# Modulation and the compressed keys' first layer as products on quarters of TensorE's array, and all rests on VectorE, in a two-block network on one core

## The chip, the cores and the metric

One core of a Trainium2 chip runs the whole program in one launch. TensorE multiplies matrices (PE, its weight loads PEld), VectorE (DVE), ScalarE (ACT) and GpSimd (POOL) work element by element, and SyncE (SP) issues the loads. The metric is the device time of one execution in microseconds, the median of the runs.

## The reference

256 tokens of width 1024 go through two blocks. Only the first one is touched here. In it a condition vector `c` is turned into six modulation vectors by one product of a vector with a matrix of 1024 x 6144 (24 MB):

```
cond = silu(c)
mod = cond @ ada_w + ada_b
sh1, sc1, g1, sh2, sc2, g2 = split(mod, 6)
h = rms_norm(x, ln1_g) * (1 + sc1) + sh1
x = x + g1 * hybrid_mixer(h, w_in, w_out, ...)
h = rms_norm(x, ln2_g) * (1 + sc2) + sh2
x = x + g2 * sparse_moe(h, ...)            # 32 experts, 4 per token
```

So `sc1` and `sh1` are needed ahead of everything, `g1` at the output projection, `sc2` and `sh2` at the routing, `g2` at the end of the experts. The mixer holds two kinds of attention over the same projection `w_in`. One of them attends, among others, to compressed keys and values: 31 windows (two groups of 15, and the position vectors as one more column) of 32 x 64 numbers each go through `gelu(flat @ w1) @ w2`, with `w1` of 2048 x 128, once for keys and once for values.

All is fp32. A dense product of activations and weights is made of three products of rounded parts, hi x hi, hi x lo and lo x hi.

## The kernel before, in words

**Weights.** Class `Stream` loads 1 MB tiles of weights in one fixed list order (`add`, `pump`; the load is L170). The list is written by hand at the head of the kernel: `add_ada(s, q)` puts a quarter (256 rows by 1024 columns) of section `s` of `ada_w` into it, `more(n)` the next `n` quarters of the sections that are not yet in it. There are four places of 1 MB and some more in stretches (`widen`). A load can start when the tile that was in its place, and all tiles ahead of that one, are used. A tile of dense weights is cut into two units; `split_to` makes each unit's hi part on ScalarE (L190) and its rest, lo, by a subtraction (L192) on GpSimd or VectorE; the letters of `st.cut` say which, in turn. `st.ahead` says how many units ahead this is done. Modulation's tiles are used as they are (`get_raw`).

**Order on the engines.** Each engine runs its instructions in the order in which the program writes them. A dense step `dense_t` writes 24 products (three per 128 rows of weights: L290, L291, L292) into one bank `dps`, and between them pops other work: attention steps (`self.bg`, by `fill`) and one part of the side list `self.side` (by `aux`); `side_to(n)` writes parts until `n` are left. A part of the side list that needs a tile is not popped before its load is written.

**Modulation (`ada`).** Per section eight parts, one for each 128 rows of `ada_w`. VectorE multiplies a row of 1024 columns per partition by that partition's condition and adds it up in `acc` (L435 the first, L437 the others); in some parts ScalarE multiplies (L429, L557) and GpSimd adds (L431, L560). Then two totals: four transposes of 128 columns on TensorE (L449), a sum over their columns on VectorE (L452), and the addition to the bias (L454). Sections 1 and 0 come ahead of the first dense product (with an extra form of the last quarter, L592); the other four are the side list and go on until the second half of the output projection, where `side_to` writes what is left.

**Compressed keys.** `hid_part` multiplies, in eight background steps of four products (L660), 128 x 128 weights with 31 columns of the windows.

**Stages on the time line:** start to 41.2 us; two dense steps for the compressed keys and values and six for queries and keys of the first kind of attention, to 80; gates and values to 94; eight dense steps for queries and keys of the second kind with attention between them (L727, L741 norms; L830, L834 scores; L837 to L859 softmax; L866 transposes into the banks `tp` and `m`; L877 and L880 values, L880 for two heads in the upper and the lower 64 partitions of one bank), to 158; two steps of values to 190; output projection (`w_out_half`, eight banks each, with the update of h, L949, after each bank), first half to 217, second with the routing's products (L1032, L1035) to 250; routing to 263; the experts (first product L1441) to 1208; the second block to the end.

The lines 1914 and 1915, in the second block, are two products inside a loop over two heads, so that the program writes L1914, L1915, L1914, L1915; the two heads write the upper and the lower 64 partitions of one bank:

```
for a in range(2):
    hs = slice(64 * a, 64 * a + 64)
    mm(ot[hs, META:NT], lhsT=v[:, 64 * a:64 * a + 64], rhs=wa[:, a], ...)          # L1914
    mm(ot[hs, META + 128:NT], lhsT=v[:, 128 + 64 * a:192 + 64 * a], rhs=wb[:, a], ...)  # L1915
```

Of the kernel before, what the change touches and what calls it, by code (L numbers as in the profile page):

```python
# [20 lines left out]
S = 256  # L21
# [222 lines left out]
class Ker:  # L244
# [116 lines left out]
    def queue_pre(self):  # L361
# [14 lines left out]
        for s in (1, 0):  # L376
            for q in range(4):
                add_ada(s, q)
        add_cols(st, w, 512, 256)
        cw = A["nsa_cmp_w1"][0]  # L380
        for c in range(2):
# [4 lines left out]
                    for m in range(2)])  # L386
            st.add([(lambda t, b=b: t.rearrange("p (l h) -> p l h", l=16)[64 * b:64 * b + 64],
                     cw[c, 1024 * b:1024 * b + 1024].rearrange("(l d) h -> d l h", d=64)) for b in range(2)], ["raw"])
        for o in (768, 896):
# [5 lines left out]
            more()  # L395
        self.early = len(st.items)
        for c in range(4):
            add_cols(st, w, 1304 + 256 * c, 256)
            more(2 - c % 2)
        for c in range(2):  # L400
            st.add([(_v("p (k n) -> p k n", k=8), w[:, 2328 + c * 256:2584 + c * 256].rearrange("(k p) n -> p k n", p=128))],
                   [lambda t, m=m: t[:, m * 1024:m * 1024 + 1024] for m in range(2)])
            more()
        wo = A["w_out"][0]
        for c in range(2):
# [4 lines left out]
            more()  # L410
        for c in range(2):
            add_half(st, wo[:, c * 512:c * 512 + 512], 512, 512)
        more(len(rest))

    def ada(self, s, acc, pool, tag, first=0):

        nc = self.nc
        accs = [acc]

        def part(k):  # L420
            def go():
                if k % 2 == 0:
                    self.ada_t = self.st.get_raw()
                t, used = self.ada_t
                w = t[:, (k % 2) * 1024:(k % 2) * 1024 + 1024]
                if k in (1, 3, 5) and self.mid is not None:

                    b, t = self.mid[:, 0], self.mid[:, 1]
                    nc.scalar.activation(out=t if len(accs) > 1 else b, in_=w, func=AF.Copy, scale=self.cond[:, k:k + 1])  # L429
                    if len(accs) > 1:  # L430
                        nc.gpsimd.tensor_tensor(out=b, in0=b, in1=t, op=ALU.add)  # L431
                    else:
                        accs.append(b)
                elif k == first:
                    nc.vector.tensor_scalar(out=acc, in0=w, scalar1=self.cond[:, k:k + 1], scalar2=None, op0=ALU.mult)  # L435
# [7 lines left out]
        def total(i):  # L443
            def go():
                ps = pool.tile([128, 512], F32, name="adat", tag=tag)
                if len(accs) > 1:
                    nc.vector.tensor_tensor(out=acc, in0=acc, in1=accs.pop(), op=ALU.add)
                for m in range(4):
                    nc.tensor.transpose(ps[:, m * 128:m * 128 + 128], acc[:, i * 512 + m * 128:i * 512 + m * 128 + 128],  # L449
                                        self.c("ident"))  # L450
                t = self.pp.tile([128, 4], F32, name="adas", tag="adas", bufs=2)
                nc.vector.tensor_reduce(out=t, in_=ps.rearrange("p (m n) -> p m n", m=4), axis=AX.X, op=ALU.add)  # L452
                m4 = self.mod[:, 8 * s + 4 * i:8 * s + 4 * i + 4]
                nc.vector.tensor_tensor(out=m4, in0=t, in1=m4, op=ALU.add)  # L454
            return go

        return [part(k) for k in range(8)] + [total(i) for i in range(2)]
# [42 lines left out]
    def pre(self):  # L500
# [4 lines left out]
        with ExitStack() as ctx:  # L505
# [39 lines left out]
            self.mid = None  # L545
# [1725 lines left out]
```

## Time and profile before

| | us |
|---|---|
| median of 3 runs | 1894.74 (1891.46 to 1902.87) |
| profiled execution | 1895.64 |
| its span | 1893.8 |
| TensorE busy | 1776.0 (94%) |
| VectorE busy | 991.1 (52%) |
| ScalarE busy | 632.8 (33%) |
| GpSimd busy | 410.2 (22%) |
| TensorE's mean granted clock | 0.976 |

The span runs from the first to the last instruction. A busy share over the whole span mixes stages with different limits, so the stretches of the rows below are to be read one by one. A granted clock of 1.00 is TensorE's higher level (2.4 GHz), 0.50 its lower one (1.2 GHz). One fp32 product is two records of TensorE (two passes).

### The profile page before, as it was taken

To read this page: it belongs to the slowest core of one execution; us is meant where nothing else is said; L and a number is where in the kernel's file an instruction comes from. 1 tells how busy PE (TensorE), PEld (TensorE's weight loads), DVE (VectorE), ACT (ScalarE), POOL (GpSimd) and SP (SyncE) were. 2 spreads that over 40 slices of the span, in tenths; PEclk is the share of its full clock that TensorE was granted. 3 is DMA by queue.
4 is the path that set the end of the run, shared out by engine and by line. 5 is a ranking of instruction groups with operands and counts; after the bars stand their busy time and mean duration, and the time that the engine had idled before them with its cause. 6 is when DMAs were issued, how large, how long until landed. Compare 5 with 4: busy or idle time off the path is not lost. (4 is left out here: it accounts for less than half of the span.)

```text
span 1893.8 us, 25887 instructions
## 1 busy us (share of the span) xinstructions
PE 1776.0 (94%) x10035; PEld 1107.9 (58%) x10035; DVE 991.1 (52%) x1617; ACT 632.8 (33%) x1110; POOL 410.2 (22%) x269
## 2 busy tenths in 40 slices
PE   3988779999999999999999999799999999889998
PEld 2866643333334343333434333377779999889986
DVE  7686744544444433444443444545566543996622
ACT  3444322111211101121110112346565544756633
POOL 4533310000000000000000000164433344554443
PEclk6999989999999999999999999899999999999999
DMA  9544789999999999999999999552245545346552
GB/s 342 205 149 135 251 326 370 424 425 424 424 425 423 425 425 401 424 424 425 423 426 424 400 424 424 222 175 74 74 134 175 182 157 178 112 128 181 181 188 79
DMA packets 183342, 549.60 MB, mean 290 GB/s; under 512 B 8656, under 2 KB 101968, under 8 KB 150256
## 3 DMA queue, kind: packets, MB, share of 16 engines
q1 hardware_dynamic: 182592, 545.99, 74.5%
q0 software_dynamic: 432, 1.57, 0.3%
q8 instruction: 80, 1.31, 0.3%
q10 hardware_dynamic: 192, 0.35, 0.1%
q14 instruction: 46, 0.38, 0.1%
HBM read 546.83 MB, written 1.05 MB: 289 GB/s over the span
## 5 line engine op out<-in xcount | busy, mean ns | idle before, releaser
L192 POOL TENSOR_TENSOR wsp<-wraw,wsp 128x1024 fp32r<-128x1024 f32 x137 | 337.1, 2465 | 1383.8 <-PE cb L1568 964.6
L190 ACT CAST wsp<-wraw 128x1024 fp32r<-128x1024 f32 x208 | 215.4, 1044 | 108.8 <-PE f L2184 46.9
L290 PE MATMUL dps<-hn_hi,wsp 128*128 128x272 f32 (+1 forms) x816 | 242.8, 297 | 9.5 <-DVE h L1935 4.1
L291 PE MATMUL dps<-hn_lo,wsp 128*128 128x272 f32 (+1 forms) x816 | 237.1, 291 | 4.0 <-DVE hn_lo L1637 4.0
L292 PE MATMUL dps<-hn_hi,wsp 128*128 128x272 f32 (+1 forms) x816 | 237.4, 291 | 0.8 <-DVE wsp L192 0.8
L1572 DVE SCALAR_TENSOR_TENSOR h<-cb,vec,h 128x256 f32<-128x256 f32 x256 | 111.8, 479 | 227.5 <-PE cb L1568 227.5
L1441 PE MATMUL u<-wraw_s,xs 128*64 128x512 f32 x728 | 208.5, 602 | 0.9 <-DVE gl L1471 0.9
L1469 ACT COPY gl<-u 64x512 f32<-64x512 f32 x120 | 66.8, 583 | 418.0 <-PE u L1441 357.0
L1441 PE MATMUL u<-wraw,xs 128*64 128x512 f32 x648 | 195.2, 604 | 0.0
L290 PEld LDWEIGHTS dps<-hn_hi,wsp 128*128 128x128 f32 x816 | 157.4, 193 | 14.7 <-issue 5.8
L1441 PE MATMUL u<-wraw_r,xs 128*64 128x512 f32 x544 | 164.4, 608 | 0.0
L291 PEld LDWEIGHTS dps<-hn_lo,wsp 128*128 128x128 f32 x816 | 157.3, 193 | 5.4 <-DVE hn_lo L1637 4.7
L292 PEld LDWEIGHTS dps<-hn_hi,wsp 128*128 128x128 f32 x816 | 157.3, 193 | 1.1 <-DVE wsp L192 1.1
L1471 DVE TENSOR_TENSOR gl<-u,gl 64x512 f32<-64x512 f32 x120 | 79.1, 680 | 140.9 <-ACT gl L1469 140.9
L192 DVE TENSOR_TENSOR wsp<-wraw,wsp 128x1024 fp32r<-128x1024 f32 x71 | 91.2, 1287 | 90.6 <-ACT wsp L190 90.5
L1441 PEld LDWEIGHTS u<-wraw_s,xs 128*64 128x64 f32 x728 | 54.7, 136 | 75.4 <-issue 66.2
L2035 DVE TENSOR_TENSOR y<-r 128x272 f32<-128x272 f32 (+1 forms) x64 | 53.5, 835 | 62.6 <-ACT r L2032 62.6
L1441 PEld LDWEIGHTS u<-wraw,xs 128*64 128x64 f32 x648 | 49.5, 136 | 60.4 <-issue 51.5
L1543 PE MATMUL y<-wraw_s,at 128*64 128x512 f32 x368 | 82.8, 594 | 0.0
L1543 PE MATMUL y<-wraw_r,at 128*64 128x512 f32 x336 | 78.0, 605 | 3.7 <-SPq L1246 3.7
L1567 PE MATMUL cb<-st,y 128*128 128x256 f32 x256 | 80.2, 336 | 0.1
L1510 ACT COPY at<-at_ps 128x512 f32<-128x512 f32 x34 | 19.9, 587 | 176.9 <-PE at_ps L1508 176.9
(514 smaller groups left out, 3325.4 us busy)
## 6 DMA issues: line engine op xcount, KB each, us to landing
wraw_s<-in_exp_w SPq DMA_DIRECT2D x147, 1024.0 KB, 14.3
wraw_r<-in_exp_w SPq DMA_DIRECT2D x120, 1024.0 KB, 15.4
wraw<-in_exp_w SPq DMA_DIRECT2D x117, 1024.0 KB, 14.1
wraw<-in_mlp_w_up SPq DMA_DIRECT2D x32, 1024.0 KB, 5.4
wraw<-in_mlp_w_down SPq DMA_DIRECT2D x32, 1024.0 KB, 4.8
wraw<-in_ada_w SPq DMA_DIRECT2D x18, 1024.0 KB, 5.9
wraw<-in_sb_w_qkv SPq DMA_DIRECT2D x12, 1024.0 KB, 4.9
wraw<-in_lru_w_in SPq DMA_DIRECT2D x8, 1024.0 KB, 5.0
```

The lines of the kernel that those rows point to most:

```text
L190: nc.scalar.copy(out=hv, in_=src)
L192: e.tensor_tensor(out=lv, in0=src, in1=lr, op=ALU.subtract)
L290: mm(o, lhsT=wh, rhs=xh, start=first, stop=False)
L291: mm(o, lhsT=wh, rhs=xl, start=False, stop=False)
L292: mm(o, lhsT=wl, rhs=xh, start=False, stop=last)
L1441: mm(u[n][64 * j:64 * j + 64], lhsT=xs[:, k, o:o + 64], rhs=w[:, ns], start=(q == 0), stop=(q == 3))
L1469: nc.scalar.copy(out=o, in_=u[n][64:128])
L1471: nc.vector.tensor_tensor(out=o, in0=u[n][R], in1=o, op=ALU.add)
L1543: mm(y[n][64 * j:64 * j + 64], lhsT=at[:, k, 0:64], rhs=w[:, ws], start=(q == 0), stop=(q == 3))
L1567: mm(o, lhsT=yh[:, m * 128:m * 128 + 128], rhs=st, start=True, stop=False)
L1572: nc.vector.scalar_tensor_tensor(out=h[:, m, META:NT], in0=o, scalar=self.mod[:, 40 + m:41 + m], in1=h[:, m, META:NT], op0=ALU.mult, op1=A ...
L2035: nc.vector.tensor_tensor(out=y[:, :n], in0=r[:, :n], in1=r[:, :n], op=ALU.mult)
```

## The change

Each tile of modulation becomes eight products on TensorE instead of sums on VectorE. The condition of 128 rows, one column repeated 32 times, is the stationary side, 256 columns of the tile are the moving side, and the output goes to one of four quarters (32 partitions) of one bank. Two rows of weights per tile and four column blocks make eight products. VectorE then copies or adds the 256 columns into `acc`. A total is two small products with a choice matrix that picks one partition of each quarter. The compressed keys' first layer gets the same form: the windows are the stationary side (32 columns), `w1` the moving side (128 columns), the sixteen products go round the four quarters, and a product with `sel` adds the quarters up and turns them. All rests of the first block go to VectorE. In the load order the first `w_in` tile comes between sections 1 and 0, the compressed keys' `w1` after `w_in`'s fifth tile, and the side sections earlier; all side parts are written before the output projection. The norm of the start moves from GpSimd to VectorE.

```diff
-        for s in (1, 0):
-            for q in range(4):
-                add_ada(s, q)
+        for q in range(4):
+            add_ada(1, q)
         add_cols(st, w, 512, 256)
+        for q in range(4):
+            add_ada(0, q)
...
-            more()
+            for c in range(2):
+                if o == 768:
+                    st.add([(lambda t, b=b: t.rearrange("p (l h) -> p l h", l=16)[64 * b:64 * b + 64],
+                             cw[c, 1024 * b:1024 * b + 1024].rearrange("(l d) h -> d l h", d=64)) for b in range(2)], ["raw"])
+        more(3)
         self.early = len(st.items)
         for c in range(4):
             add_cols(st, w, 1304 + 256 * c, 256)
-            more(2 - c % 2)
+            more(3 - c // 2)
...
-        def part(k):
+        def part(q):
             def go():
-                if k % 2 == 0:
-                    self.ada_t = self.st.get_raw()
-                t, used = self.ada_t
-                w = t[:, (k % 2) * 1024:(k % 2) * 1024 + 1024]
...
-                    nc.vector.scalar_tensor_tensor(out=acc, in0=w, scalar=self.cond[:, k:k + 1], in1=acc,
-                                                   op0=ALU.mult, op1=ALU.add)
-                if k % 2:
-                    used()
+                t, used = self.st.get_raw()
+                if q == 0 or not whole:
+                    st["ps"] = bank("adap")
+                ps = st["ps"][:, 0:256]
+                for i in range(2):
+                    c = self.cond[:, 2 * q + i:2 * q + i + 1].to_broadcast([128, 32])
+                    for j in range(4):
+                        o = i * 1024 + j * 256
+                        nc.tensor.matmul(ps[32 * j:32 * j + 32], lhsT=c, rhs=t[:, o:o + 256],
+                                         start=(i == 0 and (q == 0 or not whole)), stop=(i == 1 and (q == 3 or not whole)))
+                used()
+                if whole and q < 3:
+                    return
+                x = self.acc[:, s % 2]
+                if whole or q == 0:
+                    nc.vector.tensor_copy(out=x, in_=ps)
+                else:
+                    nc.vector.tensor_tensor(out=x, in0=ps, in1=x, op=ALU.add)
...
+        def total():
+            ps = bank("adat")
+            sel = self.c("ident").rearrange("p (j a) -> p j a", j=4)[:, :, 0]
+            for b in range(2):
+                nc.tensor.matmul(ps[:, 4 * b:4 * b + 4], lhsT=self.acc[:, s % 2, b * 128:b * 128 + 128], rhs=sel, start=True,
+                                 stop=True)
+            m8 = self.mod[:, 8 * s:8 * s + 8].rearrange("p (j b) -> p b j", b=2)
+            nc.vector.tensor_tensor(out=m8, in0=ps[:, 0:8].rearrange("p (b j) -> p b j", b=2), in1=m8, op=ALU.add)
...
-            self.rsqrt(rs[:, 0], self.ss[:, :S], rs[:, 1], rs[:, 2], nc.gpsimd)
+            self.rsqrt(rs[:, 0], self.ss[:, :S], rs[:, 1], rs[:, 2])
...
-                nc.gpsimd.tensor_tensor(out=xT[:, k], in0=h[:, k, X], in1=rs[:, 0], op=ALU.mult)
+                nc.vector.tensor_tensor(out=xT[:, k], in0=h[:, k, X], in1=rs[:, 0], op=ALU.mult)
...
+            self.st.cut = "D"
+            self.st.split_to(2)
+            self.st.ahead = 2
...
+            self.ada_bank = pa, "tp"
+            for s in (2, 4, 3, 5):
+                self.side += [(k < 4, f) for k, f in enumerate(self.ada(s))]
...
-                for l in range(4 * q, 4 * q + 4):
-                    nc.tensor.matmul(ps[:, 0:31], lhsT=w1[:, l], rhs=kc[i][:, l], start=(l == 0), stop=(l == 15))
+                for l in range(16):
+                    j = l % 4
+                    nc.tensor.matmul(ps[32 * j:32 * j + 32, 0:128], lhsT=kc[i][:, l], rhs=w1[:, l], start=(l < 4),
+                                     stop=(l >= 12))
+        def hid_turn(i):
+            def go():
+                ps = self.ps_m.tile([128, 512], F32, name="hid", tag="m")
+                nc.tensor.matmul(ps[:, 0:32], lhsT=state["hid", i], rhs=sel, start=True, stop=True)
+                hidden(i, ps)
...
-        self.bg = [hid_part(i, q) for i in range(2) for q in range(4)] + [nop] * 4 + [ckeys, nop, nop, nop, cnorm]
+        self.bg = [nop] * 10 + [hid_part(0), hid_part(1), hid_turn(0), hid_turn(1), nop, nop, ckeys, nop, nop, nop, cnorm]
         for i in range(6):
-            self.dense_t(0, H, L, S, ev_norm(0, i, 6), min(i, 1))
+            self.dense_t(0, H, L, S, ev_norm(0, i, 6), i // 4)
+            if i == 1:
+                self.st.ahead = 4
...
-        self.st.cut = "P"
         for i in range(8):
-            self.dense_t(0, H, L, S, ev_norm(1, i, 8), 2 if i % 4 < 2 else 1)
+            self.dense_t(0, H, L, S, ev_norm(1, i, 8), 2)
...
-        self.mid = self.ar("s3", [128, 2, 1024], F32, "mid2")
-        self.side_to(28)
+        self.side_to(15)
...
         w_out_half(0, lambda m: None)
         self.fill(len(self.bg))
-        self.side_to(21)
+        self.side_to(0)
...
-        self.st.cut = "DP"
         w_out_half(4, self.route_tile)
...
-        self.aux()
-        if m > 3:
-            self.st.cut = "P"
-        if m == 5:
-            self.side_to(11)
+        if m == 1:
             self.route_bias()
...
-        self.side_to(0)
         self.st.limit = None
```

In the line numbers of the changed kernel the side products are L437, the totals L454, the copies and additions L444 and L446, the totals' addition L457, the scores L815 and L819, the norms' product L710, h's update L932.

TensorE in the eight dense steps of the second kind of attention, between two dense products (scores, then a norm's product). Before:

```order
L830 LDWEIGHTS identb
L830 MATMUL sc<-alibi,identb 128x384
L830 LDWEIGHTS identb
L830 MATMUL sc<-alibi,identb 128x384
L834 MATMUL sc<-z 128x128 x2
L834 MATMUL sc<-z 128x256 x2
L290 MATMUL dps<-hh,wsp 128x256
L291 MATMUL dps<-hl,wsp 128x256
L292 MATMUL dps<-hh,wsp 128x256
L727 MATMUL hs<-sq,once 32x256
```
Now:

```order
L815 LDWEIGHTS identb
L815 MATMUL sc<-alibi,identb 128x384
L815 LDWEIGHTS identb
L815 MATMUL sc<-alibi,identb 128x384
L819 MATMUL sc<-z 128x128 x2
L819 MATMUL sc<-z 128x256 x2
L437 MATMUL adap<-wraw,cond 32x256 x8
L290 MATMUL dps<-hh,wsp 128x256
L291 MATMUL dps<-hl,wsp 128x256
L292 MATMUL dps<-hh,wsp 128x256
L710 MATMUL hs<-sq,once 32x256
```
The eight products of a side tile stand between the scores and the next dense products; twelve of the sixteen side tiles come so in these steps, the four others in the six steps ahead and in the value steps.

VectorE in the first half of the output projection, from its sixth bank on (`ol` the rest of the attention's output). Before:

```order
L437 SCALAR_TENSOR_TENSOR acc<-wraw,cond,acc 128x1024
L949 SCALAR_TENSOR_TENSOR h<-dps,vec,h 128x256
L286 TENSOR_TENSOR ol<-ot,oh 128x256
L437 SCALAR_TENSOR_TENSOR acc<-wraw,cond,acc 128x1024
L949 SCALAR_TENSOR_TENSOR h<-dps,vec,h 128x256
L447 TENSOR_TENSOR acc<-acc,mid_1658 128x1024
L452 TENSOR_REDUCE adas<-adat 128x4
L454 TENSOR_TENSOR vec<-adas,vec 128x4
L949 SCALAR_TENSOR_TENSOR h<-dps,vec,h 128x256
L452 TENSOR_REDUCE adas<-adat 128x4
L454 TENSOR_TENSOR vec<-adas,vec 128x4
```
Now:

```order
L286 TENSOR_TENSOR ol<-ot,oh 128x256
L853 COPY ap<-tp 128x384
L932 SCALAR_TENSOR_TENSOR h<-dps,vec,h 128x256
L192 TENSOR_TENSOR wsp<-wraw,wsp 128x1024
L286 TENSOR_TENSOR ol<-ot,oh 128x256
L932 SCALAR_TENSOR_TENSOR h<-dps,vec,h 128x256 x2
L192 TENSOR_TENSOR wsp<-wraw,wsp 128x1024
```
The sums (L437, L447), sums over transposes (L452) and additions (L454) between the updates of h are gone; subtractions for the weights' rests (L192) stand among them.

VectorE at the start, ahead of the first dense product. Before:

```order
L574 SCALAR_TENSOR_TENSOR a_198<-vec 128x8
L435 TENSOR_SCALAR acc<-wraw,cond 128x1024
L437 SCALAR_TENSOR_TENSOR acc<-wraw,cond,acc 128x1024
L582 TENSOR_TENSOR acc<-acc,mid 128x1024
L437 SCALAR_TENSOR_TENSOR acc<-wraw,cond,acc 128x1024 x2
L592 SCALAR_TENSOR_TENSOR acc<-wraw_r_149,cond,acc 128x512 x4
L452 TENSOR_REDUCE adas<-adat 128x4
L454 TENSOR_TENSOR vec<-adas,vec 128x4
L452 TENSOR_REDUCE adas<-adat 128x4
L454 TENSOR_TENSOR vec<-adas,vec 128x4
```
Now:

```order
L305 TENSOR_TENSOR rs_146<-rs_146 128x256
L553 TENSOR_TENSOR xs_154<-h,rs_146 128x256 x8
L444 COPY acc<-adap 128x256
L457 TENSOR_TENSOR vec<-adat,vec 128x2x4
L558 SCALAR_TENSOR_TENSOR a_212<-vec 128x8
L192 TENSOR_TENSOR wsp<-wraw,wsp 128x1024 x2
L444 COPY acc<-adap 128x256
L457 TENSOR_TENSOR vec<-adat,vec 128x2x4
L572 SCALAR_TENSOR_TENSOR hl<-xs_154,vec,hh 128x256 x8
```
The sums over `wraw` are gone; the norm's products with x (L553), two rests, and for each section one copy (L444) and one addition (L457) stand in their place.

## Rows read from the trace of the kernel before

**Rows 1.** Busy time by stage: PE, PEld, DVE, ACT, POOL; clock; DMA share, GB/s.

```profile
94.20:158.10 63.90, 56.33 (x409) 42.07 (x408) 51.65 (x114) 29.69 (x99) 19.54 (x8) 1.00 0.50 163
158.10:189.80 31.70, 27.10 (x174) 19.58 (x174) 19.66 (x39) 10.96 (x31) 14.73 (x13) 1.00 0.36 106
189.80:208.90 19.10, 17.38 (x124) 13.05 (x124) 13.25 (x34) 10.77 (x28) 5.99 (x3) 0.91 0.31 103
208.90:223.10 14.20, 7.72 (x52) 7.28 (x50) 11.48 (x13) 4.07 (x5) 9.21 (x4) 0.88 0.95 325
223.10:250.20 27.10, 21.05 (x156) 19.31 (x154) 20.52 (x26) 4.92 (x11) 6.92 (x2) 0.94 0.90 356
...
262.80:300.80 38.00, 36.68 (x160) 13.84 (x161) 13.72 (x28) 5.25 (x9) 0.00 (x0) 0.97 0.82 312
300.80:1208.00 907.20, 897.53 (x4079) 352.31 (x4075) 403.93 (x696) 151.47 (x211) 0.00 (x0) 1.00 1.01 420
1208.00:1893.80 685.80, 644.53 (x4474) 585.07 (x4474) 383.45 (x544) 367.81 (x620) 304.44 (x201) 0.98 0.44 141
```

**Rows 2.** Timeline of the start: start, length, engine, instruction, [idle before, releaser].

```profile
10.24 0.75 DVE L435 TENSOR_SCALAR acc<-wraw_r,cond 128x1024 f32<-128x1024 f32 x1 [3.97 <-DMA wraw_r<-in_ada_w]
...
20.19 1.15 ACT L557 ACTIVATE mid<-wraw,cond 128x1024 f32<-128x1024 f32 x1 [5.03 <-DMA wraw<-in_ada_w]
...
38.46 1.08 PE L449 MATMUL adat<-cst,acc 128*128 128x128 f32 x4 [14.84 <-DVE acc L592]
...
41.22 0.58 PE L290 MATMUL dps<-hh,wsp 128*128 128x256 f32 x1 [0.22 <-ACT hh L601]
```

**Rows 3.** Timeline of PE, one block of the compressed keys' products.

```profile
51.14 1.01 PE L660 MATMUL hid<-vvt,wraw 128*128 128x31 f32 x8
51.98 0.37 PE L290 MATMUL dps<-hh,wsp 128*128 128x256 f32 x1
```

**Rows 4.** Timeline of PE around a 32-column product (L727).

```profile
62.04 0.28 PE L292 MATMUL dps<-hh,wsp 128*128 128x256 f32 x1
62.25 0.62 PE L727 MATMUL hs<-sq,once 128*32 128x256 f32 x2
62.80 0.39 PE L290 MATMUL dps<-hh,wsp 128*128 128x256 f32 x1
63.02 0.28 PE L291 MATMUL dps<-hl,wsp 128*128 128x256 f32 x1
63.14 0.29 PE L292 MATMUL dps<-hh,wsp 128*128 128x256 f32 x1
```

**Rows 5.** Timeline of PE, products on the array's column halves.

```profile
1272.91 0.66 PE L1914 MATMUL ot<-wa,vnat 128*64 128x256 f32 x4
1273.39 0.40 PE L1915 MATMUL ot<-wb,vnat 128*64 128x128 f32 x4
```

**Rows 6.** Timeline of PE, L877 on the whole array, L880 on column halves.

```profile
116.51 0.59 PE L877 MATMUL ot<-ap 128*128 128x256 f32 x2
117.03 0.87 PE L880 MATMUL ot<-ap,vvt 128*64 128x256 f32 x8
117.83 0.39 PE L290 MATMUL dps<-hh,wsp 128*128 128x256 f32 x1
```

**Rows 7.** Timeline of PE, four transposes of modulation.

```profile
99.28 0.60 PE L449 MATMUL adat<-cst,acc 128*128 128x128 f32 x4
99.64 0.37 PE L290 MATMUL dps<-hh,wsp 128*128 128x256 f32 x1
```

**Rows 8.** Timeline of the output projection.

```profile
207.73 9.50 SPq L170 DMA_DIRECT2D wraw<-in_ada_w  x4
...
214.77 3.14 DVE L447 TENSOR_TENSOR acc<-acc,mid 128x1024 f32<-128x1024 f32 x1
...
218.06 1.09 PE L449 MATMUL adat<-cst,acc 128*128 128x128 f32 x4 [4.78 <-DVE acc L447]
```

**Rows 9.** PE's waits from 94.2 to 158.1: total, times, longest.

```profile
PE sc L830 <- ACT ap L848: 4.7, 4, 1.8
```

More of the change, by code (lines that the diff above doesn't have):

```diff
@@ L402, in queue_pre @@
                    [lambda t, m=m: t[:, m * 1024:m * 1024 + 1024] for m in range(2)])
-            more()
+            more(2 - c)
         wo = A["w_out"][0]
@@ L409, in queue_pre, with ada @@
                    [lambda t, m=m: t.rearrange("p (k n) -> p k n", k=4)[:, :, m * 256:m * 256 + 256] for m in range(2)])
-            more()
         for c in range(2):
             add_half(st, wo[:, c * 512:c * 512 + 512], 512, 512)
-        more(len(rest))
-    def ada(self, s, acc, pool, tag, first=0):
+        assert not rest
+    def ada(self, s, whole=None):
         nc = self.nc
-        accs = [acc]
-        def part(k):
-            def go():
-                if k % 2 == 0:
-                    self.ada_t = self.st.get_raw()
-                t, used = self.ada_t
-                w = t[:, (k % 2) * 1024:(k % 2) * 1024 + 1024]
[L426 to L435, printed above, removed]
-                else:
-                    nc.vector.scalar_tensor_tensor(out=acc, in0=w, scalar=self.cond[:, k:k + 1], in1=acc,
-                                                   op0=ALU.mult, op1=ALU.add)
-                if k % 2:
-                    used()
-            return go
[L443 to L457, printed above, removed]
@@ new lines, in ada, with bank @@
+        st = {}
+        def bank(name):
+            pool, tag = whole or self.ada_bank
+            return pool.tile([128, 512], F32, name=name, tag=tag)
+        def part(q):
+            def go():
+                t, used = self.st.get_raw()
[14 more added lines that the diff above has]
+                    nc.vector.tensor_copy(out=x, in_=ps)
+                else:
+                    nc.vector.tensor_tensor(out=x, in0=ps, in1=x, op=ALU.add)
+            return go
@@ L459, in aux @@
+        return [part(q) for q in range(4)] + [total]
     def aux(self, n=1):
@@ L604, in pre @@
             self.side = []
-            for s, a in ((2, 0), (4, 1), (3, 0), (5, 1)):
-                self.side += [(k in (0, 2, 4, 6), f) for k, f in enumerate(self.ada(s, acc[a], self.ps_m, "m"))]
-            self.side.insert(-2, (False, lambda: None))
+            self.ada_bank = pa, "tp"
+            for s in (2, 4, 3, 5):
+                self.side += [(k < 4, f) for k, f in enumerate(self.ada(s))]
             self.mixer(lambda k: hh[:, k], lambda k: hl[:, k])
@@ L638, in mixer @@
             nc.vector.tensor_scalar(out=gain8[:, j:j + 1], in0=self.V(nm), scalar1=0.125, scalar2=None, op0=ALU.mult)
-        kc = [x[:, 0:496].rearrange("p (l n) -> p l n", l=16) for x in (self.k0, self.k1)]
+        kc = [x.rearrange("p (l n) -> p l n", l=16) for x in (self.k0, self.k1)]
+        for x in kc:
+            nc.gpsimd.memset(x[:, :, 31:32], 0.0)
+        sel = pp.tile([128, 32], F32, name="sel32")
+        nc.vector.tensor_reduce(out=sel, in_=ident.rearrange("p (j r) -> p r j", j=4), axis=AX.X, op=ALU.add)
         def ev_cmp(i, ps):
```

58 lines of the change are left out of this document (12 added, 46 removed).

## The prediction

> **What bounds the kernel now.** I read the busy time by stage first, because an average over the span mixes three programs. From 300.8 us to 1208 the transfers are busy all the time (share 1.01, 420 GB/s): the experts' weights set the pace there. From 1208 on TensorE is busy 644.53 of 685.80 us, in code that the change does not touch [rows 1]. So nothing in those 1593 us moves by itself; what matters is when they begin. Between 262.8 and 300.8 TensorE is busy 36.68 of 38.00 and the transfers stand at 0.82: the first expert's tiles wait for buffers that TensorE gives back. I conclude that a shift of the first expert product passes to the end one for one. What is left is the 262.8 us before it.
>
> In that part TensorE is the bound by work in the two attention stages (56.33 of 63.90, 27.10 of 31.70), but not around the output projection: 7.72 of 14.20 and 21.05 of 27.10, at granted clocks of 0.88 and 0.94 [rows 1]. The timeline says who holds it. Before the first dense product, at 41.22, it has done next to nothing for the modulation: the transposes at 38.46 had waited 14.84 us for VectorE's weighted sums [rows 2]. In the projection one addition on VectorE (L447, 3.14 us beside GpSimd) keeps the next transposes, and all products queued behind them, for 4.78 us [rows 8].
>
> **The sum, term by term** (gains negative).
>
> *Start.* A 1 MB tile lands every 2.49 us: tile 1 is first read at 10.24, tile 5 at 20.19 [rows 2]. In the new order the ninth tile completes the two sections that the first product needs, so it is there at 10.24 + 8 x 2.49 = 30.2. Behind it stand its products (2.1: the streaming of the price below at half clock, and the change of shape), a copy of 128x256 (no row of its own here; I take 0.6), and the chain of a total, from its products to the first dense product. Now that chain is 2.76 (38.46 to 41.22 [rows 2]) and holds a sum over columns that goes out; I take 1.8. 34.7 instead of 41.22: **-6.5**. Bounds: -9 if TensorE, busier than now, has its full clock by then; -2 if a tile of w_in or a rest on VectorE comes late.
>
> *Compressed keys.* Eight blocks of eight records leave the dense stream. One costs 51.98 - 51.14 = 0.84 [rows 3] and 0.10 more, by which the dense product after such a group is late (0.22 at 62.80 where 0.12 is usual, 63.02 to 63.14 [rows 4]): 8 x 0.94 = 7.5. In come per tensor sixteen products of 128 columns on quarters, four rounds of two passes, 0.9 at 0.11 each, a change of shape of 0.3 (below), and a turn of 0.2: 2.8 for both, with the tail. **-4.5**.
>
> *Transposes.* 32 in the side work, 0.36 per four [rows 7] and 0.10 as above: 8 x 0.46 = 3.6 out. Four totals of two small products come in, 0.25 each: **-2.6**.
>
> *The sixteen side tiles*, 128 products now in TensorE's queue, are the one new cost. No row shows four quarters. The nearest is the 32-column product L727 (256 columns, two passes). From the dense product ahead of it at 62.04 to the second one after it at 63.02 there are 0.98; two dense products at 0.12 of that, so it costs 0.74 [rows 4]. Over the whole array two such passes (L877) take at most 0.52, and the eight passes of L880 on two column halves, four of 256 columns and four of 128, go by in 0.80 (117.03 to 117.83) [rows 6]. So a pass streams for about 0.22, half of that for 128 columns: 0.44 of the 0.74 are streaming and about 0.3 is the change of shape and back; and the halves run together, for in turns L880 would need 4 x 0.22 + 4 x 0.11 = 1.3. If four do so too, a tile is two rounds of two passes, 4 x 0.22 = 0.9, and 0.3: 1.2. Lower bound 0.9 (no change of shape), upper 16 x 0.22 + 0.3 = 3.8 (one quarter at a time). I take 1.2, since the halves show nearly the full gain: 16 x 1.2 = **+19.2**.
>
> *Eight-dense stage.* Its idle time is 7.6 [rows 1], of which 4.7 waits for ScalarE's exponentials behind VectorE's maxima [rows 9]. VectorE loses ten 128x1024 sums and GpSimd all rests, but VectorE gets eight rests and twelve short additions, and each modulation tile now shares the one bank "tp" with the attention's transposes. I take half of the 4.7 off and 0.7 on: **-1.6** (between -7.6 and +12, the latter 1 us at each of twelve tiles). The two value stages, idle for 4.6, lose the sums and additions too: **-2.1** (0 to -4).
>
> *Output projection.* All side work is done by then. The 14.2 us from 208.9 hold 52 records [rows 1], ten of them transposes and the like, 42 dense products of 0.12: 5.0, and 0.2 for a late update: -9.0. From 223.1, 27.1 us: 21.05 busy, less three totals (1.4) and what the granted clock of 0.94 cost in it (0.06 x 27.1 = 1.6), and nearly no idle time: 18.0, -9.1. From 189.8 a wait behind a sum, -1.2. These contain four totals (1.8) that I have already counted: **-17.5**. What is late next is VectorE's update of h from each bank, or ScalarE's cast of the next weights; twelve products per bank (1.4) cover both, and without that cover I would lose up to 4 here.
>
> The loads' order itself I cost at nothing: the transfers' share in the mixer is 0.3 to 0.5 [rows 1]. GpSimd is left idle there; nobody waits for it.
>
> Sum: -6.5 - 4.5 - 2.6 + 19.2 - 1.6 - 2.1 - 17.5 = -15.6. The profiled execution took 1895.64 (span 1893.8), so **1880**; it stands 0.9 over the median of the three runs, which I neglect.
>
> **Rivals.**
>
> 1. *Quarters overlap half.* An fp32 product is two passes. If TensorE starts passes strictly in program order, a quarter's second pass waits for its first and holds the next quarter: 8 x 0.22 + 0.3 = 2.1 per tile, +14.4, and 2 for the keys: **1896**. The trace speaks against it: the program alternates L1914 and L1915 (lines 1914 and 1915, over two heads), the trace starts all of L1914 first [rows 5], so one half's product does not wait for the other's. The Trainium skill, "TensorE: Matmul & The Clock Gate", section "Part 3: Packing small matmuls", says that MATMULs are "strict FIFO, no reordering"; by that rule this rival would be the forecast, and the trace differs here.
>
> 2. *Slower than before: one quarter at a time.* At 3.8 per tile the mixer pays 16 x 2.6 = 42 more than I count, the start 8 x 1.3 = 10 (eight tiles of 3.8 that land every 2.49), the keys 5: **1937**. It turns into a loss from about 2.1 per tile on, where 16 x 0.9 and the keys eat the sum. For it: no row shows more than two column positions, and all quarters write one bank. Against: halves lose nothing in one bank.
>
> 3. *VectorE's queue.* It takes the rests from GpSimd, and a rest (128x1024) may stand before a maximum or an addition that frees bank "tp". At the twelve tiles of the eight-dense stage 1 us each, about the mean of the four waits there now (4.7 in 4 [rows 9]): **1892**. For it: VectorE is the second busiest there, 51.65 of 63.90 [rows 1]. Against: it gives up more than it gets.
>
> 4. *Prefetch.* The transfers are at 0.95 and 0.90 in the projection [rows 1]; if the experts' first tiles don't come earlier, only the room of the four modulation tiles loaded there [rows 8] is won: 4 x 2.49 = 10 of 17.5, **1888**. Against: those tiles leave this stretch, so the transfers have as much less to do in it as TensorE.
>
> 5. *All ends good.* Tiles at 0.9 (-5), idle 4 less, full clock at the start (-2.5), no wait left in the projection (-2): **1866**.
>
> That the change doesn't reach its place can be left out: the order of instructions shows the side products where I count them.
>
> **How the numbers follow.** Forecast 0.52, own range 1870 to 1889; rival 5 0.20; rival 1 0.11; rival 3 0.09; rival 2 0.04; rival 4 0.04. The range 1863 to 1898 leaves out rival 2, the far end of 5 and some of 1 and 3: under 0.2. One per cent (what a measurement of this kernel can tell) is 19 us, so faster by more means under 1876: rival 5 and a third of the forecast, 0.39. Slower by more means over 1914: rival 2 and what several mishaps together give, 0.09. Within: 0.52.
>
> **What would show it.** First dense product at 34 to 35; eight L437 products of a tile within 1.2 us between two dense products, in rounds of four near starts (2.1 or 3.8 tell rivals 1 and 2); no wait of TensorE over 1 us in the projection, which should take 41 us where 189.8 to 250.2 is 60.4 now; the eight-dense stage 74 to 78 us long; first expert product near 247, and the same distance of 1631 us from there to the end. I am wrong if that distance grows (rival 4), or if waits for "tp" or VectorE add up to more than 6 us in the eight-dense stage (rival 3).

## The result, and the profile after

Slower: median 1911.6 us of 20 runs (1895.41 to 1915.23) against 1893.05 of 20 runs of the kernel before (1891.33 to 1903.48); ratio 1.0074, 95% interval 1.0058 to 1.0091. The forecast was 1880, the range 1863 to 1898. The prediction gave 0.52 to a time within one per cent (19 us) of the kernel before; that came, at 18.6 us, but by luck, since the forecast lay 15 us on the other side. The profiled execution took 1911.35 (span 1909.6). The runs of the kernel before lie in two groups, near 1892 and near 1902 us; beside e5 to e8 below, nine of 16 were in the upper one, which makes those four ratios some 0.3% lower than against 1893.

The stages, each measured between the same instructions of both traces:

| stage | before, us | after, us | difference | forecast |
|---|---|---|---|---|
| start to the first dense product | 41.2 | 35.6 | -5.6 | -6.5 |
| compressed keys, first kind, to the first value product | 41.8 | 42.9 | +1.1 | -2.1 |
| gates and first values, to the eight dense steps | 11.3 | 23.7 | +12.5 | +2.4 |
| eight dense steps | 64.5 | 88.0 | +23.5 | +11 |
| second values | 31.1 | 36.5 | +5.3 | -2 |
| output projection, to its last product block | 58.2 | 41.6 | -16.7 | -18 |
| routing, to the first expert product | 14.7 | 14.7 | 0 | 0 |
| from there to the end | 1631.0 | 1626.6 | -4.4 | 0 |

(The forecast's column splits its terms by place, two side tiles in the second stage, two in the third, twelve in the fourth.) The stretches of the changed kernel, with the columns of [rows 1]:

```profile
35.60:78.50 42.90, 39.60 (x332) 33.39 (x333) 24.80 (x61) 24.77 (x53) 3.04 (x10) 0.91 0.94 288
78.50:102.20 23.70, 17.00 (x96) 10.81 (x94) 6.24 (x11) 3.11 (x5) 0.00 (x0) 0.77 0.28 88
102.20:190.20 88.00, 77.35 (x610) 53.17 (x606) 43.89 (x123) 30.25 (x99) 0.00 (x0) 0.91 0.61 192
190.20:226.70 36.50, 34.49 (x170) 24.83 (x169) 16.26 (x37) 10.82 (x30) 0.00 (x0) 0.72 0.24 86
226.70:252.20 25.50, 22.46 (x167) 18.48 (x167) 16.66 (x40) 10.05 (x28) 0.00 (x0) 0.93 0.12 43
252.20:268.30 16.10, 15.88 (x139) 15.67 (x138) 5.73 (x14) 3.06 (x5) 2.83 (x1) 1.00 0.95 357
268.30:283.00 14.70, 6.83 (x40) 5.27 (x38) 8.57 (x35) 7.70 (x21) 5.29 (x7) 0.63 0.81 323
283.00:1225.00 942.00, 933.57 (x4237) 365.59 (x4238) 416.41 (x724) 156.55 (x220) 0.00 (x0) 1.00 1.00 414
```

The third column from the right is the granted clock. It was 1.00 in the eight dense steps and in the second values of the kernel before [rows 1]; it is 0.91 and 0.72 now, and 0.77 in the first values, where TensorE is busy for only 17.00 of 23.70 us. The projection does what was forecast in time (22.46 of 25.50, 15.88 of 16.10 at a clock of 1.00 in its second half), but not without a wait over 1 us:

```profile
241.13 1.92 PE L865 MATMUL ot<-ap,vvt 128*64 128x256 f32 x8 [3.04 <-DVE ol L286]
```

L286, 0.42 us, stood on VectorE behind a rest (238.30) that had waited 2.07 us for its cast.

TensorE at the start of the changed kernel, where [rows 2] stood:

```profile
14.27 2.80 PE L437 MATMUL adap<-wraw_r,cond 128*32 128x256 f32 x48
...
31.25 1.94 PE L437 MATMUL adap<-wraw_r,cond 128*32 128x256 f32 x16 [0.55 <-DMA wraw_r<-in_ada_w]
33.74 1.01 PE L454 MATMUL adat<-cst,acc 128*128 128x4 f32 x4 [0.55 <-DVE acc L444]
35.61 0.58 PE L290 MATMUL dps<-hh,wsp 128*128 128x256 f32 x1 [0.86 <-ACT hh L571]
```

Three tiles (48 records; a tile is eight products of two passes) go by in 2.80 us, 0.93 per tile; a tile at the lower clock takes 1.94. First dense product at 35.61.

The first values, all engines (SPq issues the loads):

```profile
83.69 1.07 PE L437 MATMUL adap<-wraw,cond 128*32 128x256 f32 x16
...
84.69 0.38 PE L494 MATMUL dps<-wsp,hh 128*128 128x256 f32 x1
...
84.82 0.37 SPq L170 DMA_DIRECT2D wraw<-in_w_in  x1
...
89.88 1.99 ACT L190 CAST wsp<-wraw 128x1024 fp32r<-128x1024 f32 x2 [10.79 <-DMA wraw<-in_w_in]
90.96 2.36 DVE L192 TENSOR_TENSOR wsp<-wraw,wsp 128x1024 fp32r<-128x1024 f32 x2 [5.71 <-ACT wsp L190]
93.23 0.47 DVE L726 SCALAR_TENSOR_TENSOR z<-z,gain,hb 128x256 f32<-128x256 f32 x1
...
93.76 1.22 PE L724 MATMUL hb<-hr,spread 32*128 32x256 f32 x2 [6.58 <-DVE z L726]
```

A side tile takes 1.00 (83.69 to 84.69). As soon as it is used its place is free, and at 84.82 the load of the next dense tile is issued (SyncE had waited 11.2 us for that). It lands for ScalarE's cast at 89.88. Behind the cast are two rests on VectorE, and behind these, in VectorE's queue, the 0.47 us of L726, whose result empties the bank that TensorE's next product L724 needs. TensorE waits 6.58 us. What its clock does then, in stretches of 4 us (the granted clock again third from the right):

```profile
83.00:87.00 4.00, 4.00 (x34) 2.53 (x32) 0.90 (x2) 0.00 (x0) 0.00 (x0) 1.00 0.26 50
87.00:91.00 4.00, 0.18 (x2) 0.00 (x0) 0.04 (x1) 1.12 (x2) 0.00 (x0) 1.00 0.60 212
91.00:95.00 4.00, 1.24 (x3) 0.59 (x3) 2.71 (x3) 0.87 (x1) 0.00 (x0) 0.54 0.17 26
...
111.00:115.00 4.00, 4.00 (x26) 2.67 (x26) 1.86 (x7) 0.80 (x3) 0.00 (x0) 0.50 0.21 39
115.00:119.00 4.00, 4.00 (x41) 2.92 (x41) 0.43 (x1) 0.64 (x2) 0.00 (x0) 0.97 0.86 291
```

The clock falls in the stretch that follows the wait and stays at 0.50 until the one before 115. Then the second such stretch, 197 to 217 us. First the second values of the kernel before, then those of the changed one (six value products stand between two rows of each, the same program):

```profile
168.35 0.69 PE L741 MATMUL hb<-hr,spread 32*128 32x256 f32 x2
...
169.88 0.69 PE L741 MATMUL hb<-hr,spread 32*128 32x256 f32 x2
```

```profile
200.65 1.22 PE L724 MATMUL hb<-hr,spread 32*128 32x256 f32 x2
...
203.37 1.22 PE L724 MATMUL hb<-hr,spread 32*128 32x256 f32 x2
```

1.53 us from row to row at the higher clock, 2.72 at the lower one. The changed kernel came to it after a wait of 1.3 us at 193, behind a rest again (L192 at 192.82, 1.21 us, ahead of the copy L853). The products ran at the higher clock for 2.6 us more, then the clock fell and came back at 217, in the middle of the stage, after a block of scores. And in the eight dense steps:

```profile
PE tp L851 <- DVE acc L446: 4.9, 2, 3.4
PE adap L437 <- ACT ap L855: 2.9, 2, 1.7
PE tp L851 <- DVE acc L444: 0.8, 1, 0.8
```

The attention's transposes (tp) wait for additions into `acc` that must empty the bank they share with the side tiles: 4.9 us in two waits, 2.9 the other way round. The longest one, 3.4 us up to 175.65, has no late load in it: the addition stood behind a rest that had waited 3.0 us for ScalarE's cast, and the cast behind the exponentials (so the expectation of e1 below names the wrong reason for this wait).

### The profile page after: what moved, and what is told of

The parts are those of the page before. It is cut to its first block, busy times and chain, and to the rows that moved or that the text cites. A ratio compares the mean times of both kernels' runs of the same rounds, so it can differ in the third digit from the quotient of the medians.

```text
span 1909.6 us, 26541 instructions
## 1 busy us (share of the span) xinstructions
PE 1811.4 (95%) x10399; PEld 1123.8 (59%) x10399; DVE 932.8 (49%) x1612; ACT 624.9 (33%) x1103; POOL 317.5 (17%) x229
## 5 line engine op out<-in xcount | busy, mean ns | idle before, releaser
L192 POOL TENSOR_TENSOR wsp<-wraw,wsp 128x1024 fp32r<-128x1024 f32 x115 | 278.2, 2423 | 1287.4 <-PE cb L1545 958.8
L1418 PE MATMUL u<-wraw_r,xs 128*64 128x512 f32 x648 | 195.2, 604 | 0.0
L192 DVE TENSOR_TENSOR wsp<-wraw,wsp 128x1024 fp32r<-128x1024 f32 x95 | 120.0, 1271 | 118.4 <-ACT wsp L190 118.1
L1418 PE MATMUL u<-wraw,xs 128*64 128x512 f32 x544 | 164.7, 609 | 0.0
L1418 PEld LDWEIGHTS u<-wraw_r,xs 128*64 128x64 f32 x648 | 49.5, 136 | 61.5 <-issue 52.4
L1544 PEld LDWEIGHTS cb<-st,y 128*128 128x128 f32 x256 | 47.9, 187 | 51.1 <-issue 41.1
L1422 PEld LDWEIGHTS u<-b,P 64*64 64x64 f32 (+1 forms) x128 | 16.8, 132 | 103.4 <-issue 103.4
```

What stands on the lines that cost most here:

```text
L192: e.tensor_tensor(out=lv, in0=src, in1=lr, op=ALU.subtract)
L1418: mm(u[n][64 * j:64 * j + 64], lhsT=xs[:, k, o:o + 64], rhs=w[:, ns], start=(q == 0), stop=(q == 3))
L1544: mm(o, lhsT=yh[:, m * 128:m * 128 + 128], rhs=st, start=True, stop=False)
```

## The experiments

Theory A: the products on quarters cost what they should; the loss is VectorE's queue, in which a rest that waits for a late load now stands ahead of short steps, and TensorE's clock, which falls behind such a wait and does not come back for 20 us. Theory B: the products on quarters and the shared bank are themselves the cost. A ratio is to runs of the kernel before that were taken beside the run; their median was 1899.91 beside e5 to e8 and 1893 to 1894 beside the others.

| | change | median us | ratio to before (95%) |
|---|---|---|---|
| after | | 1911.60 | 1.0074 (1.0058 to 1.0091) |
| e1 | rests on GpSimd as before | 1893.36 | 1.0000 (0.9986 to 1.0014) |
| e2 | dense tile's load earlier | 1917.95 | 1.0135 (1.0121 to 1.0150) |
| e3 | first wait filled | 1900.11 | 1.0024 (1.0004 to 1.0045) |
| e4 | e1 and e2 | 1897.97 | 1.0020 (1.0006 to 1.0034) |
| e5 | both waits filled | 1893.18 | 0.9977 (0.9958 to 0.9996) |
| e6 | e1, its wait filled | 1884.48 | 0.9922 (0.9894 to 0.9950) |
| e7 | e1, norms three places later | 1883.96 | 0.9931 (0.9900 to 0.9962) |
| e8 | e7, another bank | 1882.73 | 0.9918 (0.9889 to 0.9946) |
| e9 | weights cut two units ahead | 1898.23 | 1.0012 (0.9987 to 1.0037) |
| e10 | e9 with e8's two repairs | 1890.61 | 0.9984 (0.9964 to 1.0003) |
| e11 | e8, later rests on VectorE | 1889.40 | 0.9965 (0.9947 to 0.9984) |

**e1, the rests undone.**

```diff
-            self.st.cut = "D"
...
+        self.st.cut = "P"
         for i in range(8):
             self.dense_t(0, H, L, S, ev_norm(1, i, 8), 2)
...
+        self.st.cut = "DP"
         w_out_half(4, self.route_tile)
...
+        if m > 3:
+            self.st.cut = "P"
```

> The change with one part undone: the first block's rests go to GpSimd and VectorE as in the kernel before; quarters and load order stay. Theory A (VectorE's queue and the clock): in the changed kernel a rest that waits for a late load stands on VectorE ahead of a short step that TensorE needs (waits of 2.5, 6.6 and 3.4 us at 55, 87 and 172 us), and behind the second of them, and again from 197 us, TensorE runs at its lower clock for 24 and 20 us. With the rests on GpSimd the waits go, the eight-dense stage begins near 90 instead of 102, and the time is 1880 to 1892. Theory B (the products on quarters and the shared bank are themselves the cost): nothing of that moves, 1905 to 1915, and slower steps on VectorE beside GpSimd may add to it.

18 us less than the changed kernel, just over A's range and far from B's: equal to the kernel before. The eight dense steps begin at 94.8 instead of 102.2, at the higher clock. But the second stretch at the lower clock is still there, 185 to 209 us, and the timeline says from where:

```profile
179.13 1.03 ACT L190 CAST wsp<-wraw 128x1024 fp32r<-128x1024 f32 x1
...
180.24 2.41 POOL L192 TENSOR_TENSOR wsp<-wraw,wsp 128x1024 fp32r<-128x1024 f32 x1 [2.54 <-ACT wsp L190]
...
180.47 2.46 DVE L305 TENSOR_TENSOR hr<-hr 32x256 f32<-32x256 f32 x1
...
182.86 0.54 DVE L852 COPY ap<-tp 128x384 f32<-128x384 f32 x1
...
183.45 0.69 PE L723 MATMUL hb<-hr,spread 32*128 32x256 f32 x2 [2.19 <-DVE ap L852]
```

Beside a rest on GpSimd (2.41 us) L305 on VectorE lasts 2.46 us, and 0.41 without one; the copy out of the bank comes late, TensorE waits 2.19. So the same place has a wait with either engine, for another reason.

**e2, the load order.**

```diff
-        more(3)
+        more()
         self.early = len(st.items)
...
-            more(3 - c // 2)
+            more(3)
```

> The change with two numbers of the load order altered: one modulation tile instead of three ahead of the fifth dense tile of w_in (columns 1304), three after each of the four that follow. Rests stay on VectorE. Theory A: that tile's load, issued at 84.8 us in the changed kernel because its place was held by modulation tiles, is issued before 75; the wait of 6.6 us and the lower clock from 91 to 115 go: 1890 to 1900. Theory B: 1905 to 1915. If the late tile is only replaced by a later one that is late too, the wait reappears in the eight-dense stage at the same price.

Worse, and over the ranges of both theories. The wait at 87 us is gone, and the one that the last sentence named is there, with the next dense tile:

```profile
93.62 0.37 SPq L170 DMA_DIRECT2D wraw<-in_w_in  x1
...
98.61 1.04 ACT L190 CAST wsp<-wraw 128x1024 fp32r<-128x1024 f32 x1 [6.26 <-DMA wraw<-in_w_in]
99.68 1.23 DVE L192 TENSOR_TENSOR wsp<-wraw,wsp 128x1024 fp32r<-128x1024 f32 x1 [5.63 <-ACT wsp L190]
...
101.43 0.16 DVE L457 TENSOR_TENSOR vec<-adat,vec 128x8 f32<-128x8 f32 x1
...
101.66 3.59 PE L780 MATMUL csc<-kcbd,z 128*128 128x32 f32 x16 [5.82 <-DVE vec L457]
```

The load is issued at 93.62, and the addition of a modulation total on VectorE (L457, 0.16 us) comes after the rest at 101.43; TensorE waits 5.82. In both orders the load of the late tile is issued only when TensorE has used a side tile, and the rest carries that into VectorE's queue. Whether there is an order without a late tile was not shown.

**e3, the wait filled.**

```diff
+                if group == 0 and i == 2:
+                    x = pa.tile([128, 512], F32, name="warm", tag="tp")
+                    for _ in range(56):
+                        nc.tensor.matmul(x[:, 0:S], lhsT=H(0)[:, 0:128], rhs=H(0), start=True, stop=True)
                 ps = self.ps_m.tile([128, 512], F32, name="hb", tag="m")
```

> The changed kernel with 56 additional products without use (128x256, about 6.5 us) in TensorE's queue at the wait of 6.6 us at 87 us; the wait itself stays, its time is filled. Theory A with the clock as the larger part: TensorE's clock does not fall at 91, the 24 us at the lower clock go, first expert product 8 to 12 us earlier, 1899 to 1904. If the clock falls for another reason, or costs little, the time stays at 1911 or rises by what the products take beyond the wait.

By the medians 11.5 us less than the changed kernel, by adding work to it; between the two profiled executions 5.8, with the first expert product at 277.0 instead of 283.0, 6 us earlier and not 8 to 12. The same stretches as above, with the useless products:

```profile
87.00:91.00 4.00, 4.00 (x30) 3.53 (x31) 0.38 (x1) 0.00 (x0) 0.00 (x0) 1.00 0.76 225
91.00:95.00 4.00, 4.00 (x35) 4.00 (x35) 1.88 (x2) 2.00 (x2) 0.00 (x0) 1.00 0.13 41
...
111.00:115.00 4.00, 4.00 (x37) 2.30 (x36) 1.74 (x5) 1.54 (x8) 0.00 (x0) 1.00 0.92 293
```

The wait is as long as it was (8.9 us from the issue of the late load to the norm's product behind it in the changed kernel, 9.0 here); the clock doesn't fall. So the clock fell because of the wait, and this stretch of it cost some 6 to 11 us. The second stretch is still there, 191 to 212 us.

**e4, both.** The edits of e1 and e2 together.

> The change with the rests on GpSimd and VectorE as before and the altered load order together. Theory A: both causes of the waits are gone, so at least as fast as the better of the two alone, 1878 to 1890, and faster than the kernel before. Theory B: 1905 to 1915.

4.6 us more than e1 alone: with rests on GpSimd the altered order is no help either. Theory A's number for it is missed, since its remedy for the load was wrong, and since VectorE's is not the only queue that a late load can hold:

```profile
133.00 0.37 SPq L170 DMA_DIRECT2D wraw<-in_w_in  x1
...
140.79 1.04 ACT L190 CAST wsp<-wraw 128x1024 fp32r<-128x1024 f32 x1 [4.43 <-DMA wraw<-in_w_in]
...
141.74 0.47 ACT L854 COPY ap<-tp 128x384 f32<-128x384 f32 x1
...
142.27 1.94 PE L437 MATMUL adap<-wraw,cond 128*32 128x256 f32 x16 [5.31 <-ACT ap L854]
```

Here it is ScalarE's: the cast that waits for its load stands ahead of the 0.47 us of a copy that empties the side tiles' bank. TensorE waits 5.31 us, and its clock is low from 141 to 148.

**e5, both waits filled.** As e3, and the same loop with 12 products ahead of the second values' first norm's product.

> The changed kernel with products without use in both waits behind which its clock fell for long: 56 at 87 us as in e3, and 12 (1.4 us) ahead of the first norm's product of the second value stage (the wait of 1.3 us at 193 us). Theory A: the second long stretch at the lower clock (20 us, 10 lost) goes too; from e3's 1900 to 1888 to 1893, although two stretches of products without use were added. If the second stretch has another cause than that wait, it stays at 1898 to 1903.

```profile
181.68 1.59 PE L727 MATMUL warm<-hh 128*128 128x256 f32 x12
183.20 0.69 PE L729 MATMUL hb<-hr,spread 32*128 32x256 f32 x2
...
184.74 0.69 PE L729 MATMUL hb<-hr,spread 32*128 32x256 f32 x2
```

From norm to norm 1.54 now (183.20 to 184.74), the pace of the kernel before. With 68 products without use the changed kernel takes 18.4 us less by the medians, 1893.2, as much as the kernel before. (The profiled execution is the fastest of e5's ten, 1886.63; in it the first expert product is at 262.8.)

All profiles agree on this place. Where TensorE waits 1.27 to 2.19 us ahead of the stage's first norm's product (the changed kernel, e1 to e4, e9), the clock falls 1 to 3 us later and stays low for 20 to 24 us; where it waits 0.84 us or less (the kernel before, e5 to e8, e10, e11), there is no such stretch.

**e6, e7, e8: three repairs of e1.** e6: the loop of e5 with 20 products in e1. e7 and e8:

```diff
-        self.bg = [nop]
+        self.bg = [nop] * 4                                    # e7, e8
         while rest or norms:
...
-                ps = self.ps_m.tile([128, 512], F32, name="hid", tag="m")
+                ps = (pa if i else self.ps_m).tile([128, 512], F32, name="hid", tag="tp" if i else "m")   # e8
```

> e1 (rests on GpSimd as before) with 20 products without use (2.3 us) in its wait of 2.2 us ahead of the second value stage's norms, behind which its clock is low from 185 to 209. Theory A: that stretch goes, 1893.4 less 9 to 12, 1881 to 1885, faster than the kernel before. Otherwise 1892 to 1896.

> e1 with the second value stage's background steps three places later, so that useful products of the stage stand in TensorE's queue where it waited 2.2 us. Theory A: wait and stretch at the lower clock go, 1880 to 1885. If only products without use help, because the stage's later part then lacks what was moved, 1890 to 1896.

> e7 with the second half of the compressed keys' first layer in another bank (the one of the side products, free at that time), so that it need not wait for VectorE to empty the first one (3.7 us in e1, and the lower clock from 58 to 66 behind it). Theory A: 4 to 7 us less than e7, 1874 to 1880. If the stage is bound elsewhere, as e7.

All three are faster than the kernel before (their slowest run took 1888.19 us, the fastest of any of its runs 1889.81), and e6 and e7 are where they were expected: useful products in the queue do what useless ones did. e8 gives 1 us more, not 4 to 7: the wait for the bank goes (3.7 us), but two waits of 1.9 and 1.6 us stand behind it, and the clock is low from 61 to 68 instead of 58 to 66. But e8 has the quarters, the shared bank and the load order of the change, and only the rests and two places in the program are others: at 1882.73 Theory B can't be the account of the loss. e8's middle stages:

```profile
80.50:94.20 13.70, 13.30 (x97) 8.89 (x95) 4.24 (x10) 2.73 (x5) 1.24 (x1) 1.00 0.25 77
94.20:176.80 82.60, 72.18 (x606) 48.86 (x606) 41.99 (x115) 30.73 (x100) 23.89 (x18) 0.96 0.68 212
176.80:201.20 24.40, 24.31 (x164) 18.18 (x163) 12.13 (x25) 8.75 (x20) 9.70 (x4) 1.00 0.39 148
```

The two value stages take 13.7 and 24.4 us at a clock of 1.00; the eight dense steps still take 82.6. There two rests on GpSimd hold VectorE, as one did beside L447 in the kernel before [rows 8]:

```profile
111.05 4.68 POOL L192 TENSOR_TENSOR wsp<-wraw,wsp 128x1024 fp32r<-128x1024 f32 x2 [13.39 <-ACT wsp L190]
...
111.28 2.18 DVE L825 TENSOR_SCALAR am<-am 128x2 f32<-128x2 f32 x1
...
113.37 2.38 DVE L826 SCALAR_TENSOR_TENSOR am<-am 128x2 f32<-128x2 f32 x1
...
116.33 0.90 PE L850 MATMUL tp<-cst,ap 128*128 128x128 f32 x3 [3.48 <-DVE acc L446]
```

L825 and L826 last 2.18 and 2.38 us, and 0.17 and 0.21 alone; TensorE waits 3.48 for the addition queued behind them.

**e9, fewer units ahead.**

```diff
-            if i == 1:
-                self.st.ahead = 4
...
         self.side_to(15)
+        self.st.ahead = 4
```

> The changed kernel, rests on VectorE and load order as they are, with weights cut two units ahead in the mixer instead of four, so that the rest which waits for the late load at 87 us is written into VectorE's queue about one dense step later, behind the norms. Theory A (a rest on VectorE, written ahead of its load's landing, holds the short steps behind it): the wait of 6.6 us and the lower clock behind it go, 1893 to 1900 as in e3 and e1. If the load itself is what is late, the wait comes back at the eight-dense stage's first products, 1905 to 1912.

As A has it: rests on VectorE, load order as in the change, and the first wait is gone (the eight dense steps begin at 88.0), 13 us less. A wait of 2.3 us remains ahead of 92.7, at the eight dense steps' first products, with 7 us at the lower clock behind it. It is not the engine of the rest alone, but that it was put into the queue so far ahead of its load. The stretch from 182 to 206 remains.

**e10 and e11.** e10 is e9 with the two repairs of e8; e11 is e8 with `cut = "D"` from the eight dense steps on.

> e9 with the two other repairs of e8 (the second value stage's background steps three places later; the second half of the compressed keys' layer in another bank). Theory A: 8 to 14 us less than e9, since the second stretch at the lower clock goes too: 1880 to 1889. If VectorE's rests cost more than GpSimd's, it stays over e8's 1882.7.

> e8 with the rests of the eight-dense stage and of everything behind it on VectorE, as the change has them; GpSimd only takes part ahead of that. In e8 two rests on GpSimd at 111 us hold small steps of the softmax on VectorE (2.2 and 2.4 us for 0.2), and TensorE waits 3.5 us and loses its clock from 115 to 123. If that is what the stage lacks, 4 to 8 us less than e8: 1875 to 1879. If the rests on VectorE hold the same steps as long, as in the changed kernel (10 us of waits there against 9.8 in e8), 1881 to 1886.

e10 ends 7.6 us under e9 and 8 over e8, just outside its range; e11 is 6.7 over e8, outside both of its ranges. So what is left between VectorE and GpSimd, when the long stretches at the lower clock are gone, is in favour of GpSimd here, although its rests hold VectorE: in the changed kernel's eight dense steps the waits sum to some 10 us, in e8's too, and e11 gained nothing from the exchange. How much it is, and why, is open: e10 also cuts fewer units ahead than e8, and of the 7.5 us between the profiled executions of e11 and e8 3.8 lie behind the first expert product. Of the versions tried e8 is the fastest.

## Why the prediction was wrong

**The step that failed** is "The loads' order itself I cost at nothing: the transfers' share in the mixer is 0.3 to 0.5", together with the term of -2.1 for the two value stages. A share says that the transfers have time; it doesn't say when a place is free for them. The load of the dense tile was 5 us away when its rest stood at the head of VectorE's queue. The idle time of 4.6 us behind the -2.1 is that of the second value stage alone (158.1 to 189.8 [rows 1]); in the first TensorE had been busy for 11.09 of 11.20 us, so there was nothing to gain and only waits to lose by. I had asked what is queued behind a rest only in the eight dense steps (rival 3, at 1 us each), and not in the value stages, where each of TensorE's norm products hangs on one short step of VectorE. Of the 31.4 us between forecast and profiled execution 12.5 lie in the eight dense steps, 10.1 in the first value stage, 7.3 in the second and 3.2 in the stage of the compressed keys.

**What I priced at the start and in the projection, but behind no wait of the mixer, is the clock.** The waits behind VectorE in the value stages are 6.6 and 1.3 us; what the clock added to them is more: e3 and e5 take 11.5 and 18.4 us out of the time (medians; 5.8 and 24.7 between profiled executions) and shorten neither wait. By the medians 18.4 of the 31.6 us between forecast and result are this; an estimate from the trace, half of the 44.3 us that the two stretches last, is 22. Rival 3 had the right engine, and its sign came (waits of 10.0 us in the eight dense steps, where 6 was the limit); its price was little more than a third, 12 us, with no clock in it. What I held against it was true and did not help: VectorE gave up more than it got (busy for 51.65 us of the stage before, for 43.89 now), and a step can still stand behind a rest.

**The side tile at 1.2** was right: 1.00 between two dense products at the higher clock, and 13.6 us of records in e1 for the twelve of the eight dense steps (1.13 each). The records start in rounds of four, 0.02 us apart, a round every 0.22 to 0.24. Rival 1 (2.1) and rival 2 (3.8) are out. The Trainium skill's rule in "TensorE: Matmul & The Clock Gate", section "Part 3: Packing small matmuls", that MATMULs are not reordered, would have made it 2.1; the trace with four quarters differs as the one with halves did.

**Start** (-6.5) and **projection** (-17.5, with its totals) came as worked out: -5.6 and -16.7. The wait of 4.8 behind L447 is gone and the longest for h is 0.6 where it was 2.6; the sign "no wait over 1 us" failed by the 3.0 us at 241, which the sum could bear.

**Compressed keys** (-4.5): the products were right (32 records in 1.08), but the second tensor's had to wait 2.5 us for the bank of the first, which VectorE emptied behind a rest, and ran at the lower clock. The stage lost 1.1 where I had 2.1 as a gain.

**Eight dense steps:** forecast 74 to 78, measured 88.0. The first 13 us of it lie in the long stretch at the lower clock (6.5), and the waits at the shared bank "tp" are 10.0 in place of the 4.7 that I had counted down to 3. In e8, without the long stretch, it is 82.6, with waits of 9.8; they remain the mis-sized part of the -1.6. A version with another bank for the side tiles was not tried: each of the eight banks that the kernel allots holds other work.

**The stretch to the end** became 4.4 us shorter, and 8 in e8 (257.3 to 1880.4). I had argued one for one, which is near enough for the sum, but it flatters e8: its first expert product is at 257.3, 10 us later than my 247, and only the 8 us that I had counted at nothing bring it to 2.7 us over the forecast. Most of them (6.1) lie between the last product of the experts' first layer and the end, mainly the second block, which the change does not touch: 699.5 us before with 34.6 at the lower clock, 693.4 in e8 with 24.1. Why is not settled, and neither is the spread of the changed kernel (1895 to 1915 in 20 runs, where e8 has 1882 to 1884): only one execution of each has a profile.

## What to carry to other kernels

Ask of every instruction that waits for a load, a cast on ScalarE (e4) as well as a rest on VectorE, on which in-order queue it stands, what short step is behind it, and who hangs on that step; a low share of the transfers does not answer it. Then price a wait of TensorE by what its clock does afterwards, not by its length. A wait that can't be taken away can be covered: later placement of what waits (e7) cost nothing and gave 9.4 us, products without use (e6) gave 8.9.

## What the runs showed of the hardware

- The rounds of the second values (six products of 256 columns and one small norm's product) kept the level of the clock that they were on: the higher one from 166.8 to 175.9 us in the kernel before and from 183.2 to 195.4 in e5 (1.53 and 1.54 us per round), the lower one from 197.9 to 214.2 in the changed kernel (2.72 per round), though TensorE was busy in every 4.00 of 4.00 us there. It was back at the higher level at 217 after a block of scores, and in the other long stretch at 115 us.
- The length of a wait does not give its price: behind 3.4 us up to 175.65 the changed kernel's clock was low for 3.4 us (176.7 to 180.1), behind 1.3 us up to 194.55 for 20.4 (197.2 to 217.6).
- Four column quarters of TensorE run together, with two passes for each product: sixteen records of 256 columns in 1.00 us, against at most 0.52 for two over the whole array [rows 6]. So for products on different quarters "in the order in which the program writes them" is too strict: the program writes one product after the other, and four start within 0.02 us.
- Not every step of VectorE is held beside a rest on GpSimd. In e1 L305, L825 and L826 lasted up to 2.46, 1.96 and 2.39 us (alone 0.41, 0.17, 0.21), while steps that read a bank took the same beside one as alone: the copy L852 0.55 us, the addition L446 0.42, h's update L932 0.48.
